# A fused transformer step on one core: where the recurrence's head norm stands beside its output gate, and how the second feed-forward's preparation is shared among the engines

## The chip, the cores and the metric

The kernel runs on one core of one Trainium2 chip. The metric is device time in microseconds (us) of one launch; lower is better. A core has a matmul engine (PE), VectorE (DVE), ScalarE (ACT), GpSimd (POOL) and SyncE (SP, which issues the DMAs here). Each works through its own instruction queue in order, and an instruction at the head of a queue that waits holds back all that stand behind it.

## The reference

One layer of a hybrid model works on 1152 tokens (128 of a context, 1024 latent) of width 1024, in float32: a half-step feed-forward, a token mixer that adds attention and a gated linear recurrence (HGRN2), and a second half-step feed-forward. The change touches the recurrence's output and the second feed-forward:

```python
f_fw = lb_h[0] + (1.0 - lb_h[0]) * jax.nn.sigmoid(heads(hf_f, HG_DK))
o_fw, s_fw = hgrn2_chunked(q_h, 1.0 - f_fw, jnp.log(f_fw), v_h, s0[:, 0])
o_bw, s_bw = hgrn2_chunked(flip(q_h), flip(1.0 - f_bw), flip(jnp.log(f_bw)), flip(v_h), s0[:, 1])
o_rec = rmsnorm(o_fw + flip(o_bw), hg_norm_g) * jax.nn.silu(heads(hgate, HG_DV))
...
merged = jax.nn.sigmoid(ga) * (o_attn @ w_up_attn) + jax.nn.sigmoid(gr) * (o_rec @ w_up_rec)
...
x = x + 0.5 * m[2] * swiglu(modulate(x, norm_g[0], m[0], m[1]), *ffn1)
x = x + m[5] * mix
x = x + 0.5 * m[8] * swiglu(modulate(x, norm_g[2], m[6], m[7]), *ffn2)
```

Here `rmsnorm` divides by the root of a mean square, and `swiglu(h, w1, w3, w2)` is `(silu(h @ w1) * (h @ w3)) @ w2`.

## The kernel before, in words

Everything lies transposed: features on the 128 partitions, tokens along the free axis, in three blocks of 384 tokens (`CW`) or, in the second feed-forward, four quarters of 288 (`QW`). A float32 product is made of three matmuls of a narrower type (L518 to L520): each operand is split into a high part, which ACT rounds off (`xh`, `wh`, `bh`, `xd`), and a low part, the subtraction `value - high` (`xl`, `wl`, `bl`), which DVE or POOL makes. `load_w` loads a weight tile into `raw` and splits it; its argument `home` says where: `"low"` makes `wh` 128x1024 on ACT and `wl` in two halves of 128x512 on DVE (L343), none makes `wl` in one piece of 128x1024 on POOL (L351).

A scheduler places the instructions: it takes the program's order and moves what has a priority ahead (`tc.high_priority`), so the order in a queue is fixed at build time and is not that of the code. A function table of ACT is loaded where the next function isn't in the one at hand (`ACT_TABLE_LOAD`); `lnexp()` (L419) asks for the table that holds both Ln and Exp.

**The recurrence** (span 800 to 1431 us). Eight heads, made as four pairs, and woven into them the projections from `h` that everything later needs: `dense_g` (24 matmuls a block, tile `mm`), closed by `sigm` (sigmoid on ACT, tile `sg`) and, for `q` (L740) and the output gate (L800), a DVE multiply of `mm` by `sg` that also frees the matmul's bank. The scan works block by block: DVE and POOL build `QP` and `KE` with decay factors `T` (at levels of 8, 16, 32 and 64 tokens), ACT copies key halves `kr`, and PE multiplies them into `lv`. Once the four half-outputs of a pair are there (`pair["no"] == 4`), `proj_gate` of that pair squares them (`osq`), and puts `norm` on the list `later`: for each of three blocks, `rec_norm` sums the squares on PE (`ops`), `rstd` takes Ln and Exp on ACT and three `scalar_tensor_tensor` on DVE (L431 to L433), and a fourth (L1108) scales the outputs `oT`. The pairs are called 0 to 3 here; the gates of the first three run beside the next pair's scan, pair 3 after the last.

**The second feed-forward** starts at 2056 us. Its first three blocks of 256 hidden features are plain (`plain_block`): units of 24 matmuls into `ps` (L518 to L520), ACT's silu `sl` (L1763) and DVE's multiply (L1774), which frees the bank. Beside the first of them runs the last quarter (`QORDER[-1]`) of the norm, `tail`: DVE `xn` (L476), ACT's modulation (L480), a store `hd`, ACT's `bh` (L487), POOL's `bl` (L488). Its tiles `xn` come from the pool that also holds `sl`. Beside the other two run `sums`: differences `hd` (L1718 to L1721, DVE) of quarters that come back by DMA (`hb`), split into `xo` (L1724 on ACT, L1728 on DVE), the operands of seven products with sums instead of eight, used from 2144 us. The down projection (2568 to 2759 us, `down_sweep`, `down_fast`) does the same in three groups of products, each in four sweeps: it accumulates in `d` (L2044), adds to `x` and `su` on DVE (L2029, L2031, L2049), and meanwhile splits the next group's `xd` (ACT L2008; L2009 on POOL and DVE) and weights `wd` (L1983).

Of the kernel before, what the change touches and what calls it, by code (L numbers as in the profile page):

```python
# [19 lines left out]
P = 128  # L20
D = 1024
KT = D // P
# [71 lines left out]
class Trunk:  # L94
# [320 lines left out]
    def alloc_h(self):  # L415
        hl = [(self.tt(F32R, f"xh{k}"), self.tt(F32R, f"xl{k}")) for k in range(KT)]
        self.xh, self.xl = zip(*hl)

    def lnexp(self):  # L419
        self.tc.keep_in_program_order(self.nc.scalar.preload_act_table_set("natural_log_exp_and_others"))  # L420

    def rstd(self, r, ps, w=CW, out=None):
# [6 lines left out]
        nc.scalar.activation(r, ps, AF.Ln, bias=self.epst)  # L429
        nc.scalar.activation(r, r, AF.Exp, scale=-0.5)  # L430
        nc.vector.scalar_tensor_tensor(t, ps, EPS, r, ALU.add, ALU.mult)  # L431
        nc.vector.scalar_tensor_tensor(t, t, -0.5, r, ALU.mult, ALU.mult)
        nc.vector.scalar_tensor_tensor(r if out is None else out, t, 1.5, r, ALU.add, ALU.mult)  # L433
# [15 lines left out]
    def norm(self, c, i):  # L449

        nc = self.nc
        lo, hi = span(c)
        cs = slice(lo, hi)
        rs = self.rs[:, cs]
        if self.mode != "mix":
            rs = self.bank("ps1", "rsp", hi - lo)
        last = self.mode == "mix"
        if last:
            with self.tc.high_priority(offset=600):
                self.stat_end(c, rs)  # L460
        else:
            self.stat_end(c, rs)
        yield
        for k in range(KT):
            t = self.fp.tile([P, hi - lo], F32, tag=self.nt[0], bufs=self.nt[1], name="xn")
# [10 lines left out]
            nc.vector.tensor_mul(t, self.x[k][:, cs], rs)  # L476
# [10 lines left out]
            nc.scalar.copy(th, t)  # L487
            nc.gpsimd.tensor_sub(tl, t, th)  # L488
            yield

    def place(self, c):
# [222 lines left out]

    def sigm(self, ps):
        s = self.fp.tile([P, CW], F32, tag="sg", bufs=3, name="sg")
        self.nc.scalar.activation(s, ps, AF.Sigmoid)
        return s

    def proj_f(self, i, h, out):  # L720
# [14 lines left out]
    def proj_q(self, i, out):  # L735
        q = out["q"] = self.tt(F32, "q")
        w = self.load_w(self.a["w_in"][i], KT, P, home="pieces" if i == 2 else "low")
        for c in ORDER:
            ps = yield from self.proj_g(w, c)
            self.nc.vector.tensor_mul(q[:, c * CW : (c + 1) * CW], ps, self.sigm(ps))  # L740
            out["nq"] = out.get("nq", 0) + 1
            yield

# [23 lines left out]
        for f in later:  # L767
            f()

    def proj_gate(self, i, p, pair):  # L770
        nc = self.nc
        oT = pair["o"]
        assert pair["no"] == 4
        w = self.load_w(self.a["w_in"][i], KT, P, home="low")
        sq = self.tt(F32, "osq")[:, :T]
        nc.scalar.activation(sq, oT[:, :T], AF.Square)
        held, normed = [], []

        def norm():
            self.lnexp()  # L780
            for b in ORDER:
                self.rec_norm(b, oT, sq)
            normed.append(1)
            for f in held:
                f()

        def put(cs, s):
            nc.gpsimd.tensor_mul(s, oT[:, cs], s)
# [7 lines left out]
        self.later.append(norm)  # L796
        for c in ORDER:
            ps = yield from self.proj_g(w, c)
            s = self.sigm(ps)
            nc.vector.tensor_mul(s, ps, s)  # L800
            f = partial(put, slice(c * CW, (c + 1) * CW), s)
            if normed:
                f()
            else:
                held.append(f)
            yield
# [8 lines left out]
    def hgrn(self):  # L815
# [10 lines left out]
        self.cnt, self.later = 0, []  # L826
# [21 lines left out]
        def work_of(h):  # L848
            p = h // 2
            work = feed(h + 1) if h + 1 < H else []  # L850
            if h and h % 2 == 0:
                work = work + [sgs.pop(), sgs.pop()] + [self.proj_gate(5 * p - 1, p - 1, pairs[p - 1])]
            while len(work) < 4 - (h == 3) + (h == H - 1):
                work.append(sgs.pop())
            return chain(*work)
# [243 lines left out]
            d["pair"]["no"] = d["pair"].get("no", 0) + 1  # L1099
            yield  # L1100

    def rec_norm(self, c, oT, sq):
# [3 lines left out]
        nc.tensor.matmul(ps, self.onesb, sq[:, cs], start=True, stop=True)  # L1106
        self.rstd(sq[:, cs], ps)
        nc.vector.scalar_tensor_tensor(oT[:, cs], oT[:, cs], self.hg, sq[:, cs], ALU.mult, ALU.mult)  # L1108

    def attn(self):  # L1110
# [4 lines left out]
        self.lnexp()  # L1115
# [949 lines left out]
    def down_fast(self, w2, X, xg, ops, made, load_x, load_h, split_h, gm, nxt):  # L2065
# [5 lines left out]
        for g, (f, n) in enumerate(GROUPS):  # L2071
            new = {} if g else X
            last = g == len(GROUPS) - 1
            for m in range(KT // 2):
# [8 lines left out]
                def after():  # L2083
                    nonlocal k
                    if xa and k in (2, 5):
                        i, t = xa.pop(0)
                        for v in range(2):
                            c = ts(v, 2 * QW)
                            self.nc.vector.tensor_add(self.x[i][:, c], t[:, c], self.x[i][:, c])
                    if m == KT // 2 - 1 and not last:  # L2090
                        for _ in range(GROUPS[g + 1][1]):
                            next(xg, None)
                    elif last:
                        for _ in range((0, 0, 1, 2, 1, 1, 1)[k]):
                            self.folds.pop(0)()
# [24 lines left out]
    def ffn_fast(self, l, gm, nxt):  # L2120
# [9 lines left out]
        sums, ops, made = iter(()), iter(()), []  # L2130
        steps = iter(()) if l else self.whole()
        for f in range(plain):
            ws = self.pre[f] if l == 0 and f < 2 else [self.load_w(self.a["w13"][l, f, j], KT, P) for j in range(2)]
            if f == 2 - l:
                for _ in steps if l == 0 else self.tail:
                    pass
# [248 lines left out]
```

## Time and profile before

| | |
|---|---|
| runs | 2859.02, 2859.55, 2859.63 us; median 2859.55 |
| profiled execution | 2853.09 us, of which the span 2851.2 us; granted clock of PE 0.995 |
| PE busy | 2767.6 us (97%) |
| DVE, ACT, POOL busy | 2034.5 (71%), 1332.4 (47%), 967.3 us (34%) |
| ACT table loads | 39, of 1283 ns each |

Times within the program are microseconds from the start of the span. Matmuls overlap in the records: one is listed as 0.34 us, and the next starts 0.17 us behind it. A row of the timeline names the start, the length, the engine, line, operation, tiles and count, and in brackets the idle time before it with the engine, tile and line that ended it. The profiled execution ran 6.46 us below the median of the runs shown.

### The profile page before, as it was taken

The numbers are of one execution on the slowest core, as the hardware profiler recorded it, in microseconds if no ns is written. First come the engines' busy times: TensorE is split into PE (matmuls) and PEld (weight loads), VectorE is DVE, ScalarE is ACT, GpSimd is POOL, SyncE is SP. The second block draws the span as 40 slices with busy tenths as digits, with TensorE's granted clock in tenths as the row PEclk, the third lists the DMA queues.
The fourth block names the chain that finished last, engine by engine and source line by source line (L and its number), as shares of the span: only waits on it lengthen the run. The fifth ranks groups of instructions, "written<-read, shape, count | busy, mean of one in ns | idle before, by whom it ended". The sixth has DMA issues, their size and how long they took to land. (4 is left out here: it accounts for less than half of the span.)

```text
span 2851.2 us, 55762 instructions
## 1 busy us (share of the span) xinstructions
PE 2767.6 (97%) x21222; PEld 2637.0 (92%) x21222; DVE 2034.5 (71%) x4430; ACT 1332.4 (47%) x2732; POOL 967.3 (34%) x1004
## 2 busy tenths in 40 slices
PE   8999999999999999999999999899999999999998
PEld 7999999999989998899998778689989999999997
DVE  7867777677678787877356777856766665568875
ACT  6523333321176677667536787731642322235332
POOL 0133232544222222222244454433443443433450
PEclk9999999999999999999999999999999999999999
DMA  6733333743112111112512001273543443347621
GB/s 258 226 129 117 131 124 121 260 171 119 60 68 68 43 62 36 65 50 74 195 61 92 18 16 36 75 246 114 174 142 116 138 159 133 112 154 212 194 100 67
DMA packets 219579, 337.65 MB, mean 118 GB/s; under 512 B 23664, under 2 KB 141360, under 8 KB 219312
## 3 DMA queue, kind: packets, MB, share of 16 engines
q1 hardware_dynamic: 219312, 334.10, 34.9%
q8 instruction: 167, 2.74, 0.4%
q14 instruction: 100, 0.82, 0.1%
HBM read 248.47 MB, written 85.54 MB: 117 GB/s over the span
## 5 line engine op out<-in xcount | busy, mean ns | idle before, releaser
L1844 PE MATMUL b<-xo,wo 128*128 128x288 f32 x3552 | 483.6, 295 | 0.8 <-DVE wo L1819 0.8
L1844 PEld LDWEIGHTS b<-xo,wo 128*128 128x128 f32 x3552 | 475.3, 188 | 1.0 <-DVE wo L1819 1.0
L1844 PE MATMUL b<-bh,wo 128*128 128x288 f32 x1776 | 366.4, 295 | 0.0
L518 PE MATMUL mm<-xh,wh 128*128 128x384 f32 x984 | 345.2, 351 | 11.9 <-DVE sg L800 6.8
L520 PE MATMUL mm<-xh,wl 128*128 128x384 f32 x984 | 334.4, 340 | 0.0
L519 PE MATMUL mm<-xl,wh 128*128 128x384 f32 x984 | 333.7, 339 | 0.0
L547 DVE SCALAR_TENSOR_TENSOR x<-dn,modt,x 128x256 f32<-128x256 f32 (+4 forms) x472 | 226.1, 499 | 89.4 <-PE dn L520 88.0
L1844 PEld LDWEIGHTS b<-bh,wo 128*128 128x128 f32 x1776 | 289.1, 188 | 0.0
L1844 PE MATMUL b<-bl,wo 128*128 128x288 f32 x888 | 262.0, 295 | 0.0
L1818 ACT CAST wo<-raw 128x512 fp32r<-128x512 f32 x185 | 114.8, 621 | 204.0 <-PE b L1844 83.0
L518 PEld LDWEIGHTS mm<-xh,wh 128*128 128x128 f32 x984 | 186.6, 190 | 20.4 <-DVE sg L800 8.2
L2044 PE MATMUL d<-xd,wd 128*128 128x288 f32 x1344 | 181.7, 297 | 9.1 <-DVE x L2031 6.4
L2044 PEld LDWEIGHTS d<-xd,wd 128*128 128x128 f32 x1344 | 180.0, 190 | 10.7 <-ACT wd L1982 3.5
L519 PEld LDWEIGHTS mm<-xl,wh 128*128 128x128 f32 x984 | 186.7, 190 | 1.1 <-issue 0.3
L520 PEld LDWEIGHTS mm<-xh,wl 128*128 128x128 f32 x984 | 186.8, 190 | 0.0
L1819 DVE TENSOR_TENSOR wo<-raw,wo 128x512 fp32r<-128x512 f32 x185 | 127.6, 691 | 71.6 <-ACT wo L1818 69.0
L1541 POOL TENSOR_TENSOR ehl<-e,ehl 128x512 fp32r<-128x512 f32 x93 | 123.9, 1337 | 153.7 <-ACT ehl L1539 85.2
L1844 PEld LDWEIGHTS b<-bl,wo 128*128 128x128 f32 x888 | 167.4, 189 | 0.0
L390 DVE SCALAR_TENSOR_TENSOR junk<-wada,cb 128x512 bf16<-128x512 f32 x224 | 162.3, 724 | 5.8 <-DMA wada<-in_w_aT 4.9
L351 POOL TENSOR_TENSOR wl<-raw,wh 128x1024 fp32r<-128x1024 f32 (+2 forms) x48 | 95.5, 1993 | 159.0 <-ACT wh L350 153.2
L1819 DVE TENSOR_TENSOR wo<-ws,wo 128x512 fp32r<-128x512 f32 x74 | 72.2, 975 | 103.1 <-ACT wo L1818 102.9
L518 PE MATMUL ps<-bh,wh 128*128 128x288 f32 (+1 forms) x448 | 136.4, 305 | 7.4 <-DVE sl L1774 4.1
(458 smaller groups left out, 7118.8 us busy)
## 6 DMA issues: line engine op xcount, KB each, us to landing
raw<-in_w SPq DMA_DIRECT2D x148, 256.0 KB, 3.3
wada<-in_w_aT SPq DMA_DIRECT2D x112, 256.0 KB, 3.0
raw<-in_w SPq DMA_DIRECT2D x42, 512.0 KB, 3.6
raw<-in_w_in SPq DMA_DIRECT2D x41, 512.0 KB, 3.3
xr<-xd SPq DMA_DIRECT2D x56, 288.0 KB, 3.8
hr<-hs SPq DMA_DIRECT2D x26, 576.0 KB, 5.6
hb<-hd SPq DMA_DIRECT2D x44, 288.0 KB, 3.4
hs<-et SPq DMA_DIRECT2D x84, 144.0 KB, 2.2
```

Of the source, the lines that this page charges most:

```text
L351: pin((eng or self.nc.gpsimd).tensor_sub(wl, raw, wh))
L390: nc.vector.scalar_tensor_tensor(junk, ws[n % 2], 1.0, cs[s], ALU.mult, ALU.mult, accum_out=o)
L518: pin(nc.tensor.matmul(ps, wh, xh, start=start and i == 0, stop=False))
L519: pin(nc.tensor.matmul(ps, wh, xl, start=False, stop=False))
L520: pin(nc.tensor.matmul(ps, wl, xh, start=False, stop=stop and i == n - 1))
L547: nc.vector.scalar_tensor_tensor(self.x[m][:, a:b], ps[:, a - lo : b - lo], self.modt[:, gm, m, s : s + 1], self.x[m][:, a:b], ALU.mult, A ...
L1541: eng.tensor_sub(el, e, eh)
L1818: nc.scalar.copy(wh, src[i])
L1819: nc.vector.tensor_sub(wl, src[i], wh)
L1844: nc.tensor.matmul(ps, w[:, k], x[:, k, :QW], start=first, stop=last, skip_group_check=home != i)
L2044: nc.tensor.matmul(ps, w[:, k], xv, start=start, stop=stop, skip_group_check=home != i)
```

## The change

Four edits, and what they do to the order.

1. **Head norm.** `norm_gate` is cut out of `proj_gate` and is called as soon as the pair's four outputs exist, beside the merge-gate projection that runs then (`beside`). `behind` adds order-only dependencies: the roots (Ln, Exp) come behind their table load, that load behind the last twelve sigmoids, and each sigmoid behind the last six roots.
2. **Gate products.** The multiplies by `sg` for `q` and for the output gate get `high_priority(offset=150)`.
3. **Start of the second feed-forward.** The tail quarter's `xn` come from the `half` tiles, its `bl` go from POOL to DVE, and the weights of plain blocks 1 and 2 are split with `home="low"`: eight halves on DVE in place of four whole ones on POOL.
4. **Down projection.** The splits of the next group's operands are asked for two per product in the last sweep of a group (before: as many as the next group has products, 3), the rest two per product in the first sweep of the next.

```diff
+    def behind(self, ins, *first):
+        for f in first:
+            self.tc.add_manual_dep(ins.ins, f.ins.name, ...)
+        return ins
...
     def sigm(self, ps):
-        self.nc.scalar.activation(s, ps, AF.Sigmoid)
+        self.sigs.append(self.behind(self.nc.scalar.activation(s, ps, AF.Sigmoid), *self.roots[-6:]))
...
     (q projection)
-            self.nc.vector.tensor_mul(q[:, c * CW : (c + 1) * CW], ps, self.sigm(ps))
+            s = self.sigm(ps)
+            with self.tc.high_priority(offset=150):
+                self.nc.vector.tensor_mul(q[:, c * CW : (c + 1) * CW], ps, s)
...
+    def norm_gate(self, pair):
+        (square, then on the list later:)
+            table = self.behind(self.lnexp(), *self.sigs[-12:])
+            for b in ORDER:
+                self.rec_norm(b, oT, sq, table)
...
+    def beside(self, work, pair):
+        for _ in work:
+            yield
+            if pair["no"] == 4 and "held" not in pair:
+                self.norm_gate(pair)
...
-                work = work + [sgs.pop(), sgs.pop()] + [self.proj_gate(5 * p - 1, p - 1, pairs[p - 1])]
+                work = work + [sgs.pop(), self.beside(sgs.pop(), pairs[p - 1])]
+                work += [self.proj_gate(5 * p - 1, p - 1, pairs[p - 1])]
...
     (norm)
+        last, tail = self.mode == "mix", i == 2 and c == QORDER[-1]
+            if tail:
+                t = self.half("xn")[:, : hi - lo]
-            nc.gpsimd.tensor_sub(tl, t, th)
+            (nc.vector if tail else nc.gpsimd).tensor_sub(tl, t, th)
...
     (plain blocks)
-            ... [self.load_w(self.a["w13"][l, f, j], KT, P) for j in range(2)]
+            ... self.load_w(self.a["w13"][l, f, j], KT, P, home="low" if l and f else None)
...
     (down_fast)
+                    if m == KT // 2 - 1 and not last or g and not m:
+                        for _ in range(2):
+                            next(xg, None)
                     if m == KT // 2 - 1 and not last:
-                        for _ in range(GROUPS[g + 1][1]):
-                            next(xg, None)
+                        pass
```

**ACT in the recurrence, gate of pair 0.** Before, the roots (`osq`) stand between sigmoids (`sg`), each with a load of its own; this stretch begins behind the copies of the key halves `kr`:

```order
L429 ACT_TABLE_LOAD
L429 ACTIVATE osq<-ops,epst 128x384 x2
L430 ACT_TABLE_LOAD
L430 ACTIVATE osq<-osq 128x384 x2
L429 ACT_TABLE_LOAD
L429 ACTIVATE osq<-ops,epst 128x384
L717 ACT_TABLE_LOAD
L717 ACTIVATE sg<-mm 128x384
L430 ACT_TABLE_LOAD
L430 ACTIVATE osq<-osq 128x384
L717 ACT_TABLE_LOAD
```

Now they stand about 14 rows earlier, right behind the transposed keys `kT`, between two loads (their lines are now L439 and L440, and the sigmoid is L730):

```order
L1094 COPY kT<-kt 128x384
L430 ACT_TABLE_LOAD
L439 ACTIVATE osq<-ops,epst 128x384 x2
L440 ACTIVATE osq<-osq 128x384 x2
L439 ACTIVATE osq<-ops,epst 128x384
L1052 COPY kr_9106<-KE 64x24x8
L440 ACTIVATE osq<-osq 128x384
L730 ACT_TABLE_LOAD
L730 ACTIVATE sg<-mm 128x384
```

Six of the eight loads around this gate go: before there is also one of L420 and one of L717 ahead of the stretch. Pairs 2 and 3 go from eight loads to two as well; pair 1 keeps its two, and its roots move ahead by the same step. In all, 39 loads become 21. On PE only the three `ops` of pairs 0 to 2 move, to right behind the transposes `kt` (in pair 1 to behind the second of three gate blocks).

**DVE at the same place.** Before, the norm's twelve `scalar_tensor_tensor` stand behind the next block's `Kb` and `Qb`, with the gate's multiply (`sg`) in their midst:

```order
L965 TENSOR_TENSOR Kb<-kk,X 64x384
L966 TENSOR_TENSOR Qb<-qx,Y 64x384
L965 TENSOR_TENSOR Kb<-kk,Y 64x384
L966 TENSOR_TENSOR Qb<-qx,X 64x384
L431 SCALAR_TENSOR_TENSOR rt<-ops,osq 128x384 x2
L432 SCALAR_TENSOR_TENSOR rt<-rt,osq 128x384 x2
L433 SCALAR_TENSOR_TENSOR osq<-rt,osq 128x384 x2
L1108 SCALAR_TENSOR_TENSOR oT<-oT,vec,osq 128x384 x2
L800 TENSOR_TENSOR sg<-mm,sg 128x384
L431 SCALAR_TENSOR_TENSOR rt<-ops,osq 128x384
```

Now they stand some twenty rows earlier, behind the factor `Gall` and ahead of `QP` at level 16, for which PE's next `lv` waits:

```order
L1078 TENSOR_TENSOR Gall<-T_12753 128x3
L441 SCALAR_TENSOR_TENSOR rt<-ops,osq 128x384 x2
L442 SCALAR_TENSOR_TENSOR rt<-rt,osq 128x384 x2
L443 SCALAR_TENSOR_TENSOR osq<-rt,osq 128x384 x2
L1138 SCALAR_TENSOR_TENSOR oT<-oT,vec,osq 128x384 x2
L441 SCALAR_TENSOR_TENSOR rt<-ops,osq 128x384
L1077 TENSOR_TENSOR QP<-QP,T_11951 64x12x16
L442 SCALAR_TENSOR_TENSOR rt<-rt,osq 128x384
L1082 COPY_PREDICATED A_0_9112<-mask,lv 128x96
L443 SCALAR_TENSOR_TENSOR osq<-rt,osq 128x384
L1085 TENSOR_TENSOR Ad<-A_0_9112,A_9114 128x96
L1138 SCALAR_TENSOR_TENSOR oT<-oT,vec,osq 128x384
```

Nine of them are ahead of `QP`, three among what follows it. The multiplies of `q` keep their places between their neighbours.

**DVE at the start of the second feed-forward**, behind the tail's `rsp`. Before, the tail's `xn` alternate with the units' multiplies `sl`, and the first `xo` follow:

```order
L476 TENSOR_TENSOR xn<-x_21843,rsp 128x288
L476 TENSOR_TENSOR xn<-x_21879,rsp 128x288
L1774 TENSOR_TENSOR sl<-ps,sl 128x288
L476 TENSOR_TENSOR xn<-x_21917,rsp 128x288
L476 TENSOR_TENSOR xn<-x_21942,rsp 128x288
L1774 TENSOR_TENSOR sl<-ps,sl 128x288
L476 TENSOR_TENSOR xn<-x_21967,rsp 128x288
L1774 TENSOR_TENSOR sl<-ps,sl 128x288
```

Now six `xn` stand ahead of the first `sl`, and from there on the low parts of the tail (L501) and of the weights (L343) stand among the multiplies:

```order
L1804 TENSOR_TENSOR sl<-ps,sl 128x288
L501 TENSOR_TENSOR bl<-xn,bh 128x288 x2
L343 TENSOR_TENSOR wl<-raw,wh 128x512
L489 TENSOR_TENSOR xn<-x_22049,rsp 128x288
L501 TENSOR_TENSOR bl<-xn,bh 128x288 x2
L489 TENSOR_TENSOR xn<-x_22074,rsp 128x288
L1804 TENSOR_TENSOR sl<-ps,sl 128x288
L501 TENSOR_TENSOR bl<-xn,bh 128x288 x2
L343 TENSOR_TENSOR wl<-raw,wh 128x512
L501 TENSOR_TENSOR bl<-xn,bh 128x288 x2
L1804 TENSOR_TENSOR sl<-ps,sl 128x288
```

On POOL eight `bl` and the four `wl` of 128x1024 are gone there, between the weight sums `wq` which stay.

In the down projection the order differs only from the first group to the second: one 128x576 `xd` fewer stands on DVE ahead of the two `x` additions (L2031 before) that end the first group's sweeps, and it follows behind them. From the second group to the third, all queues read as before.

More of the change, by code (lines that the diff above doesn't have):

```diff
@@ L428, in rstd @@
             t = self.fp.tile([P, n], F32, tag="hf", bufs=self.hfb, name="rt")[:, :w]
[L429 to L430 removed]
+        pin(nc.scalar.activation(r, ps, AF.Ln, bias=self.epst))
+        pin(nc.scalar.activation(r, r, AF.Exp, scale=-0.5))
         nc.vector.scalar_tensor_tensor(t, ps, EPS, r, ALU.add, ALU.mult)
@@ L773, in proj_gate @@
         assert pair["no"] == 4
-        w = self.load_w(self.a["w_in"][i], KT, P, home="low")
         sq = self.tt(F32, "osq")[:, :T]
         nc.scalar.activation(sq, oT[:, :T], AF.Square)
-        held, normed = [], []
+        held = pair["held"] = []
         def norm():
-            self.lnexp()
+            table = self.behind(self.lnexp(), *self.sigs[-12:])
             for b in ORDER:
-                self.rec_norm(b, oT, sq)
-            normed.append(1)
+                self.rec_norm(b, oT, sq, table)
+            pair["normed"] = 1
             for f in held:
                 f()
+        self.later.append(norm)
+    def beside(self, work, pair):
[3 more added lines that the diff above has]
+                self.norm_gate(pair)
+    def proj_gate(self, i, p, pair):
+        nc = self.nc
+        if "held" not in pair:
+            self.norm_gate(pair)
+        oT, held = pair["o"], pair["held"]
+        w = self.load_w(self.a["w_in"][i], KT, P, home="low")
         def put(cs, s):
@@ L799, in proj_gate @@
             s = self.sigm(ps)
-            nc.vector.tensor_mul(s, ps, s)
+            with self.tc.high_priority(offset=150):
+                nc.vector.tensor_mul(s, ps, s)
             f = partial(put, slice(c * CW, (c + 1) * CW), s)
-            if normed:
+            if "normed" in pair:
                 f()
@@ L825, in hgrn @@
         self.A2 = f32("A2", [P, 3, G])
-        self.cnt, self.later = 0, []
+        self.cnt, self.later, self.sigs, self.roots = 0, [], [], []
         heads = [{} for _ in range(H)]
@@ L1100, in scan_out, with rec_norm @@
             yield
-    def rec_norm(self, c, oT, sq):
+    def rec_norm(self, c, oT, sq, table):
         nc = self.nc
@@ L1106, in rec_norm @@
         nc.tensor.matmul(ps, self.onesb, sq[:, cs], start=True, stop=True)
-        self.rstd(sq[:, cs], ps)
+        self.rstd(sq[:, cs], ps, pin=lambda i: self.roots.append(self.behind(i, table)))
         nc.vector.scalar_tensor_tensor(oT[:, cs], oT[:, cs], self.hg, sq[:, cs], ALU.mult, ALU.mult)
@@ L2132, in ffn_fast @@
         for f in range(plain):
-            ws = self.pre[f] if l == 0 and f < 2 else [self.load_w(self.a["w13"][l, f, j], KT, P) for j in range(2)]
+            ws = self.pre[f] if l == 0 and f < 2 else [
+                self.load_w(self.a["w13"][l, f, j], KT, P, home="low" if l and f else None) for j in range(2)
+            ]
             if f == 2 - l:
```

18 lines of the change are left out of this document (11 added, 7 removed).

## The prediction

> **What bounds the kernel now.** I read the page first, then the chain of waits of PE in the three stretches that the change touches.
>
> ```profile
> PE 2767.6 (97%) x21222; PEld 2637.0 (92%) x21222; DVE 2034.5 (71%) x4430; ACT 1332.4 (47%) x2732; POOL 967.3 (34%) x1004
> ```
>
> PE is the bound: outside its 2767.6 us the span of 2851.2 us holds 84 us. Nothing here takes work from PE, so the change is worth only what it takes from PE's waits. They are, in the recurrence (1000 to 1431 us), at the start of the second feed-forward (2056 to 2144) and in the down sweeps (2568 to 2759), as total, times, longest:
>
> ```profile
> PE mm L518 <- DVE sg L800: 6.8, 5, 1.8
> PE mm L518 <- DVE q L740: 3.2, 2, 2.3
> PE lv L1010 <- DVE QP L1047: 2.9, 3, 1.9
> ...
> PE ps L518 <- DVE sl L1774: 4.1, 3, 2.2
> PE ps L519 <- POOL bl L488: 2.2, 4, 1.2
> PE ps L518 <- ACT bh L487: 0.4, 1, 0.4
> ...
> PE d L2044 <- DVE x L2031: 6.4, 5, 2.5
> ```
>
> That is 12.9, 6.7 and 6.4 us. A second cost hides behind the waits. In these windows the columns are length, busy time of PE, PEld, DVE, ACT and POOL, the granted clock, DMA:
>
> ```profile
> 1053.18:1056.59 3.41, 1.56 (x41) 1.21 (x41) 2.96 (x6) 3.35 (x5) 0.21 (x1) 1.00 0.02 5
> 1056.59:1060.01 3.42, 3.42 (x12) 3.42 (x12) 2.30 (x5) 3.37 (x7) 1.95 (x4) 0.50 0.00 0
> 1203.30:1207.00 3.70, 3.70 (x81) 3.57 (x77) 3.41 (x13) 3.17 (x8) 0.50 (x1) 0.54 0.02 4
> 1319.30:1322.90 3.60, 3.51 (x11) 3.51 (x12) 2.19 (x6) 3.56 (x6) 1.99 (x4) 0.53 0.00 0
> 2121.40:2125.10 3.70, 3.70 (x19) 3.70 (x18) 1.29 (x2) 1.45 (x4) 0.00 (x0) 0.54 0.13 45
> 1414.00:1420.00 6.00, 5.00 (x29) 5.01 (x30) 3.48 (x7) 4.28 (x6) 2.60 (x3) 1.00 0.10 36
> ```
>
> PE idles 1.85 us of the first window, and through the next it has half the clock: 3.42 us that do 1.7 us of work. The same happens behind the waits at 1201, 1317 and 2118 us. Behind the wait at 1413 us it does not (clock 1.00). The waits there are:
>
> ```profile
> 1056.35 0.51 PE L518 MATMUL mm<-xh,wh 128*128 128x384 f32 x1 [1.85 <-DVE sg L800]
> 1203.17 0.45 PE L1010 MATMUL lv<-QP,kr 128*32 128x32 f32 x24 [1.88 <-DVE QP L1047]
> 1319.39 0.69 PE L518 MATMUL mm<-xh,wh 128*128 128x384 f32 x1 [1.82 <-DVE sg L800]
> 1414.99 0.44 PE L518 MATMUL mm<-xh,wh 128*128 128x384 f32 x1 [1.49 <-DVE sg L800]
> 2120.22 0.40 PE L518 MATMUL ps<-bh,wh 128*128 128x288 f32 x1 [2.16 <-DVE sl L1774]
> ```
>
> So waits of 1.82 us and more cost 1.7 us on top, 1.49 us does not, and the border lies between. I count 1.7 us where a wait falls below 1.5.
>
> The Trainium skill, "TensorE: Matmul & The Clock Gate", Part 1 (The HAM clock gate), has the half clock come after an idle window of about 3.4 us. The window's length agrees with the 3.42 us above; that it has to be idle throughout does not, as PE was busy 1.56 us of it. By that rule none of my four shortened waits would bring 1.7 us, and the sum below would be 10.8 instead of 17.6.
>
> **Head norm, pairs 0 and 2.** Why `sg` is late at 1056 us, on ACT:
>
> ```profile
> 1036.09 0.48 ACT L1064 COPY kT<-kt 128x384 f32<-128x384 f32 x1
> ...
> 1047.41 1.28 ACT L429 ACT_TABLE_LOAD   x1
> 1048.70 1.06 ACT L429 ACTIVATE osq<-ops,epst 128x384 f32<-128x384 f32 x2
> 1051.07 0.94 ACT L430 ACTIVATE osq<-osq 128x384 f32<-128x384 f32 x2
> 1053.92 1.28 ACT L717 ACT_TABLE_LOAD   x1
> 1055.22 0.49 ACT L717 ACTIVATE sg<-mm 128x384 f32<-128x384 f32 x1
> ```
>
> Four loads of 1.28 us (the first and the last of them are shown) stand in front of this sigmoid with the norm's roots between them. Afterwards all of it stands between the copies of `kT` and the first sigmoid, some 10 us earlier (`kT` is copied by 1036.57): load 1.28, Ln 1.06, Exp 0.94, Ln and Exp of the third block 1.1, a copy 0.35, load 1.28 make 6.0 us in front of the first sigmoid, where two loads of 1.28 stood. From 1036.6 us that gives the sigmoid at 1042.6, done at about 1043.1; PE ends the block before `lv` at 1043.8 and needs no bank of it sooner. The sigmoid at 1055.22 is then free to run when its matmuls end.
>
> What the twelve `scalar_tensor_tensor` now delay on DVE:
>
> ```profile
> 1042.06 0.16 DVE L1048 TENSOR_TENSOR Gall<-T 128x3 f32<-128x3 f32 x1
> 1043.83 0.40 PE L1010 MATMUL lv<-QP,kr 128*32 128x32 f32 x24
> 1044.71 2.20 PE L1106 MATMUL ops<-osq,onesb 128*128 128x384 f32 x6
> 1051.63 1.02 DVE L431 SCALAR_TENSOR_TENSOR rt<-ops,osq 128x384 f32<-128x384 f32 x2 [1.10 <-ACT osq L430]
> 1054.44 1.14 DVE L1108 SCALAR_TENSOR_TENSOR oT<-oT,vec,osq 128x384 f32<-128x384 f32 x2
> 1055.74 0.56 DVE L800 TENSOR_TENSOR sg<-mm,sg 128x384 f32<-128x384 f32 x1 [0.16 <-ACT sg L717]
> ```
>
> Eight of them took 1051.63 to 1055.58, 0.49 us each. Two `KE` multiplies step back behind them, so they begin near 1041.4 instead of 1042.2; nine at 0.49 and `QP` itself put `QP` at about 1046.2. PE wants it for the next `lv`: at 1043.83, plus the `ops` that move ahead of it (1044.71 to the next matmul at 1046.46, 1.75), so 1045.5. That is a new wait of 0.8. Behind it `Ad` and its copies hold the second sigmoid (0.15), and the multiply for the third block ends with `Kb` and `Qb` in front of it (0.4). 1.85 becomes 1.35, none of them long enough for the half clock: a gain of 0.5 + 1.7 = 2.2. Bounds: a third `mm` that waits as now while the new waits are added (-1.35), and the whole 1.85 + 1.7 = 3.55. I take the worked value. `KE` and `kr`, which also step back, serve the next block's `lv`, over 10 us later. Pair 2 reads alike: 2.2.
>
> **Pair 1** had its roots together already and only moves them some 13 us earlier. The twelve no longer meet the 1.88 us wait at 1203 us, but the chain before it (reciprocals, then `QP`) stays. Bounds 0 and 1.88 + 1.7 = 3.6; I take the middle of the wait, 1.0, and with the rest below 1.5 the clock's 1.7: 2.7. **Pair 3**: its wait of 1.49 lies behind the same loads and nothing of the scan follows that could be late: 1.5 (0 to 1.5). Recurrence: 2.2 + 2.7 + 2.2 + 1.5 = **8.6**.
>
> **Gate products.** Those of `q` keep their neighbours on DVE, so the 3.2 us on L740 stay: 0. Those of the output gate are in the sum above.
>
> **Start of the second feed-forward.** POOL's whole splits are what the quarter waits behind, and DVE slows beside them:
>
> ```profile
> L351 POOL TENSOR_TENSOR wl<-raw,wh 128x1024 fp32r<-128x1024 f32 x5 | 12.9, 2581 | 15.9 <-ACT wh L350 14.2 <-issue 1.7
> L488 POOL TENSOR_TENSOR bl<-xn,bh 128x288 fp32r<-128x288 f32 x15 | 12.9, 877 | 5.7 <-ACT bh L487 5.5
> 2060.94 2.54 DVE L1721 TENSOR_TENSOR hd<-hb,hd 128x288 f32<-128x288 f32 x1
> 2060.45 0.45 DVE L1720 TENSOR_TENSOR hd<-hb,hd 128x288 f32<-128x288 f32 x1
> 2075.49 0.98 DVE L476 TENSOR_TENSOR xn<-x,rsp 128x288 f32<-128x288 f32 x2 [5.14 <-DMA hs<-sl]
> L343 DVE TENSOR_TENSOR wl<-raw,wh x74: 678/691/1403, 859.4 to 1400.1; 128x512 fp32r<-128x512 f32 x74
> ```
>
> The same subtraction of 128x288 takes 0.45 us on DVE alone and 2.54 us beside POOL's 128x1024 split. The change drops four of those (10.3 us of POOL) and adds to DVE eight halves at 0.69 (5.5 us) and eight `bl` at 0.45 (3.6 us). The quarter's `xn` wait 5.14 us for a tile that a store of `sl` frees; from the `half` tiles they need not. The 2.2 on `bl`, 0.4 on `bh`, 4.1 on `sl` and the half clock at 2121 (1.7) make 8.4. What is late next is `sl` behind `bl` and `wl` on DVE: an `sl` with two `bl` and one `wl` in front waits up to 1.6 us, and PE sees it only when its banks run out. I leave 1.0 for that: **7.4**. Bounds: 3 (the waits on `bl` and `bh` go, the others stay) and 8.4.
>
> **Down sweeps.** Only the step from the first group to the second differs:
>
> ```profile
> 2610.78 1.56 DVE L2009 TENSOR_TENSOR xd<-xr,xd 128x576 fp32r<-128x576 f32 x1
> 2613.93 0.93 DVE L2031 SCALAR_TENSOR_TENSOR x<-d,modt,x 128x288 f32<-128x288 f32 x2
> ```
>
> One such `xd` fewer stands ahead of the `x` for which PE waits: **1.6**. Bounds: 0 (the weight split beside it ends last anyway) and 3 (the next wait shortens too). From the second group to the third: 0.
>
> **Sum.** 8.6 + 7.4 + 1.6 = 17.6 us off the profiled execution's 2853.09: 2835.5. That execution lies 6.46 us below the median of the runs shown, so the forecast in the median's terms is **2842.0**.
>
> **Rivals.**
>
> (a) *DVE becomes the limit of the gates.* Beside POOL a DVE instruction stretches (2.54 for 0.45 above); then `QP` comes 2 us later than worked out, the new wait is 2.8, and it earns the half clock that it was to save. Pairs 0 and 2 then give nothing, pair 1 about 1: the recurrence 2.5, the sum 11.5, time 2848.1. For it: nine instructions ahead of `QP` where PE has 3 us of room. Against it: POOL is nearly idle in the window at 1053 (0.21 us).
>
> (b) *The half clock stays.* It depends on where waits fall in windows of 3.41 us; if the four that I count off reappear elsewhere, 6.8 us go: 10.8 left, time 2848.8. For it: another wait of 2.3 (`q`) is still there, and shifted work meets other windows.
>
> (c) *A switch of tables costs more than its load.* If each load were followed by a pause as long again (1.28), the first sigmoid of pairs 0 and 2 would come 2.6 us later than worked out, and PE would wait about 2.2 for it; pairs 0 and 2 would give nothing, the recurrence 4.2, the sum 13.2, time 2846.4. Against it: the load at 1047.41 ends at 1048.69 and the next instruction starts at 1048.70. The Trainium skill, "ScalarE: Activation LUTs", What ACT_TABLE_LOAD costs, gives about 1283 ns for the load and 1380 ns of drain with each switch; the load agrees with the 1.28 here, and no row here shows the drain.
>
> (d) *Slower: DVE stands at the head of its queue for `wh`.* POOL waited 14.2 us on ACT's `wh` in front of its splits, where nobody stood behind. On DVE the `sl` of the units, `hd` and `xo` stand behind it. If DVE inherits the whole 14.2 and its own 5.5 and PE feels all of it, that edit costs 19.7 and the total is -19.7 + 8.6 + 1.6 = 9.5 slower: 2869. It decides from a loss of 16 us there (10.2 + 5.7). Against it: the halves stand behind instructions that themselves wait for the same units, so `wh` is mostly done.
>
> (e) *Little is changed*: table loads and splits come off engines that were idle anyhow, and PE's waits move to the next instruction. Every wait above then keeps 80% of its length: gain 3.5, time 2856.
>
> **How the numbers follow.** The forecast 0.62 (its own range 2837 to 2847), (a) 0.12, (b) 0.11, (c) 0.03, (e) 0.08, (d) 0.04. The range reaches from the sum of the upper bounds (3.55 + 3.6 + 3.55 + 1.5 + 8.4 + 3 = 23.6, or 2836) to 2853, over (a) to (c) with four microseconds of their own; it leaves out (d), (e) and the tails. A measurement of this kernel can tell about 0.2%, 5.7 us, from no change. Faster by more: the forecast and (a) to (c), 0.88; within: (e), 0.08; slower: (d), 0.04.
>
> **What would show it.** Right: 21 table loads; no half clock near 1057, 1203 and 1319; the five waits on `sg` (6.8) down to under 3; POOL without 128x1024 splits between 2065 and 2110 and no `hd` or `xo` of over 1 us there; the wait on `bl` gone. Wrong: `lv` waiting for `QP` over 1.5 us in pairs 0 and 2 (a); half clocks at new places (b); an ACT pause behind loads (c); `ps` waiting for `sl` over 5 us in all (d).

## The result, and the profile after

The changed kernel ran 2838.51 us in the median (2835.16 to 2842.20, 4 runs) against 2859.38 (2859.02 to 2859.63) of the kernel before on that chip: a ratio of 0.9928, 95% interval 0.9913 to 0.9944. On a second chip it ran 2838.02 against 2854.09: 0.9942 (0.9930 to 0.9954). The forecast was 2842.0, range 2836 to 2853. Its profiled execution took 2837.95 us, the span 2836.2, 15.0 less than before.

The page of the changed kernel, and what PE waited for in the recurrence (1000 to 1431 us), at the start of the second feed-forward (2050 to 2143) and in the down sweeps (2560 to 2755), as total, times, longest:

```profile
PE 2760.5 (97%) x21222; PEld 2630.5 (93%) x21222; DVE 2034.8 (72%) x4446; ACT 1309.2 (46%) x2714; POOL 950.3 (34%) x992
...
PE mm L531 <- DVE q L755: 4.3, 3, 2.3
PE lv L1040 <- DVE QP L1077: 3.1, 4, 1.4
PE ops L1136 <- ACT kT L1094: 1.8, 2, 0.9
PE mm L531 <- DVE sg L829: 1.4, 3, 0.8
PE dS L1102 <- ACT kT L1094: 1.1, 1, 1.1
PE vt L773 <- ACT t L766: 0.7, 1, 0.7
PE ops L1136 <- ACT osq L790: 0.5, 1, 0.5
...
PE ps L531 <- ACT sl L1793: 1.0, 1, 1.0
PE nps L515 <- DVE rs L457: 0.9, 1, 0.9
PE ps L531 <- DVE sl L1804: 0.7, 1, 0.7
...
PE d L2074 <- DVE x L2061: 4.2, 4, 2.5
PE d L2074 <- DVE su L2079: 2.0, 1, 2.0
```

The waits on `sg` fell from 6.8 to 1.4 us; those on `q` rose from 3.2 to 4.3, and 2.3 us of waits at `ops` are new. With the small rows counted too, all waits of the recurrence fell only from 14.6 to 12.9 us. At the start of the feed-forward 6.7 us became 2.6, and no `bl` is among them. PE's busy time fell by 7.1 us at the same 21222 matmuls: that is mostly half clock, which the records count as busy. Before the last matmuls there were seven windows of 3.41 us at half clock, and there are four now: two near 820 us (one before), and those near 1100 us and in the down sweeps that both kernels have. Of the four places at half clock that the prediction counted, none is left; three of them, with length, the five engines' busy times, the granted clock, DMA share and GB/s:

```profile
1053.00:1060.00 7.00, 7.00 (x74) 6.65 (x73) 6.71 (x12) 3.20 (x9) 3.81 (x5) 1.00 0.32 105
1200.00:1207.00 7.00, 5.56 (x99) 5.19 (x98) 6.60 (x18) 5.52 (x13) 1.50 (x4) 1.00 0.01 2
1316.00:1323.00 7.00, 7.00 (x73) 6.65 (x72) 6.74 (x10) 2.89 (x9) 5.24 (x6) 1.00 0.41 131
```

To see where the 15 us went, the start of the same matmul is compared in both traces (after minus before, `ops` and `kt` left out of the count):

| stretch (us of before) | at its start | at its end | gained | forecast |
|---|---|---|---|---|
| up to the recurrence, 0 to 1030 | 0 | +1.2 | -1.2 | 0 |
| pair 0, 1030 to 1110 | +1.2 | -0.5 | 1.7 | 2.2 |
| pair 1, 1150 to 1225 | -0.5 | -0.3 | -0.2 | 2.7 |
| pair 2, 1295 to 1350 | -0.3 | -2.8 | 2.5 | 2.2 |
| pair 3, 1412 to 1460 | -2.8 | -5.05 | 2.2 | 1.5 |
| second feed-forward's start, 2056 to 2143 | -5.0 | -12.2 | 7.2 | 7.4 |
| its seven-product blocks, 2143 to 2560 | -12.2 | -12.75 | 0.6 | 0 |
| down sweeps, 2560 to 2716 | -12.75 | -14.85 | 2.1 | 1.6 |

One trace stands behind each row, and two traces of one kernel differ. In `all`, the changed kernel once more (below), the first row is a gain of 1.7 instead of a loss of 1.2, pairs 0 to 3 give 1.6, -1.0, 2.5 and 2.0, and the start of the feed-forward gives 8.3.

Pair 0 in the changed kernel, on ACT, then DVE, then PE:

```profile
1037.20 0.48 ACT L1094 COPY kT<-kt 128x384 f32<-128x384 f32 x1
1037.70 1.28 ACT L430 ACT_TABLE_LOAD   x1
...
1042.02 1.28 ACT L730 ACT_TABLE_LOAD   x1
1043.31 0.49 ACT L730 ACTIVATE sg<-mm 128x384 f32<-128x384 f32 x1
...
1052.91 0.49 ACT L730 ACTIVATE sg<-mm 128x384 f32<-128x384 f32 x1
...
1042.21 1.02 DVE L441 SCALAR_TENSOR_TENSOR rt<-ops,osq 128x384 f32<-128x384 f32 x2
...
1046.98 0.36 DVE L1077 TENSOR_TENSOR QP<-QP,T 64x192 f32<-64x192 f32 x1
...
1037.73 0.91 PE L1136 MATMUL ops<-osq,onesb 128*128 128x384 f32 x2 [0.90 <-ACT kT L1094]
1048.03 0.40 PE L1040 MATMUL lv<-QP,kr 128*32 128x32 f32 x24
```

The roots stand between two loads. The sigmoid that ran at 1055.22 before runs at 1052.91, with its table long loaded. This trace runs 1.2 us behind that of before here (first row of the table), so `QP`, which ended at 1047.3, came when the prediction had it (1046.2 in the time of before). Yet `lv` does not wait: PE itself came to it only at 1048.03, some 1.3 us later than the prediction had. Of these, 0.90 is a new wait, since the third `ops` needs a bank that ACT's copy of `kT` frees. Rival (a)'s long wait of `lv` is not there (0.6 us at most in pairs 0 and 2), nor is rival (c)'s pause: the load at 1037.70 ends at 1038.98, and the next instruction starts at 1038.99.

At the start of the feed-forward POOL has one 128x1024 split left (block 0's), and DVE's subtractions there shrank. POOL's row and DVE's `xo` after, then DVE's `xo` before:

```profile
L351 POOL TENSOR_TENSOR wl<-raw,wh 128x1024 fp32r<-128x1024 f32 x1 | 2.4, 2397 | 0.3 <-POOL bl L501 0.3
...
L1758 DVE TENSOR_TENSOR xo<-hd,xo 128x288 fp32r<-128x288 f32 x32 | 15.6, 527 | 0.0
```

```profile
L1728 DVE TENSOR_TENSOR xo<-hd,xo 128x288 fp32r<-128x288 f32 x32 | 21.1, 706 | 0.0
```

The same 32 subtractions of `xo` took 21.1 us before and 15.6 after, and the difference pays for the 5.4 us of weight halves that DVE took over. Their means, 706 and 527 ns, mix. Before, 18 of the 32 met nothing on POOL and took 0.45 us each; two beside its 128x1024 splits took 2.09 and 2.62, three beside its `bl` 1.05, the others beside its smaller work 0.44 to 0.99. After, none meets a big split or a `bl`, and the longest takes 0.99.

### The profile page after: what moved, and what is told of

It reads as the page before. It is cut to its first block, busy times and chain, and to the rows that moved or that the text cites. A ratio compares the mean times of both kernels' runs of the same rounds, so it can differ in the third digit from the quotient of the medians.

```text
span 2836.2 us, 55733 instructions
## 1 busy us (share of the span) xinstructions
PE 2760.5 (97%) x21222; PEld 2630.5 (93%) x21222; DVE 2034.8 (72%) x4446; ACT 1309.2 (46%) x2714; POOL 950.3 (34%) x992
## 5 line engine op out<-in xcount | busy, mean ns | idle before, releaser
L1848 ACT CAST wo<-ws 128x512 fp32r<-128x512 f32 x74 | 45.6, 618 | 214.6 <-POOL ws L1844 214.5
```

Of the source, the lines that this page charges most:

```text
L1848: nc.scalar.copy(wh, src[i])
```

## The experiments

All are timed against the kernel before on their chip; the third column is the ratio's distance from 1 times that median.

| kernel | ratio (95%) | us against before | profiled execution |
|---|---|---|---|
| norm: edits 1 and 2 | 0.9969 (0.9958 to 0.9980) | -8.9 (-12.0 to -5.7) | 2849.37 |
| tables: norm at its old place | 0.9978 (0.9969 to 0.9987) | -6.3 (-8.9 to -3.7) | 2848.41 |
| early: place without batching | 0.9991 (0.9983 to 1.0000) | -2.6 (-4.9 to 0.0) | 2852.09 |
| ffn: edit 3 | 0.9970 (0.9958 to 0.9982) | -8.6 (-12.0 to -5.1) | 2844.57 |
| wl: weights' half of edit 3 | 0.9971 (0.9961 to 0.9981) | -8.3 (-11.1 to -5.4) | 2850.09 |
| tail: quarter's half of edit 3 | 0.9983 (0.9975 to 0.9992) | -4.9 (-7.1 to -2.3) | 2847.64 |
| down: edit 4 | 0.9996 (0.9987 to 1.0004) | -1.1 (-3.7 to +1.1) | 2854.05 |
| all: the changed kernel | 0.9942 (0.9930 to 0.9954) | -16.6 (-20.0 to -13.1) | 2838.02 |
| nop1: all, pair 1 at its old place | 0.9944 (0.9932 to 0.9957) | -16.0 (-19.4 to -12.3) | 2839.39 |
| qrec: all, reciprocals behind `q` | 0.9952 (0.9939 to 0.9965) | -13.7 (-17.4 to -10.0) | 2838.50 |
| fill: before, 9 transposes at four places | 1.0000 (0.9992 to 1.0009) | 0.0 (-2.3 to +2.6) | 2854.01 |
| fill2: the same at two places | 0.9991 (0.9982 to 1.0000) | -2.6 (-5.1 to 0.0) | 2853.44 |

The kernel before ran 2850.5 to 2860.9 us over the 70 runs beside these. The interval of one part is so wide that stretches of the traces, not totals, tell the parts apart.

**norm.** The second feed-forward and the down sweeps are put back:

```diff
-        last, tail = self.mode == "mix", i == 2 and c == QORDER[-1]
+        last, tail = self.mode == "mix", False
-                ... home="low" if l and f else None
+                ... home=None
```

> Edits 1 and 2 alone (head norm and gate products; second feed-forward as before). Theory: the recurrence keeps what the changed kernel shows there, PE 6.2 us earlier at 1460 us, of which 5.1 are three half-clock stretches that go; nothing after it differs, so the profiled execution gains about 6 to 7 us and the median as much. Rival (the parts need each other): under 3 us alone. Rival (the 6 us by which the median of before lies above its profiled execution come from the same waits): the median gains 10 us or more, the profile 6.

From 1030 to 1460 us PE gains 6.3 in its trace (from -0.25 to -6.54), as the changed kernel does (6.2). The median's gain of 8.9 (5.7 to 12.0) allows the theory and not the first rival; it does not exclude the second at its lower end.

**tables and early** take edit 1 apart.

```diff
(tables)
-                work = work + [sgs.pop(), self.beside(sgs.pop(), pairs[p - 1])]
+                work = work + [sgs.pop(), sgs.pop()]
(early, in behind)
-        for f in first:
+        for f in ():
```

> As norm, but the norm is asked for where it was before, so the three ops stand at their old places; only the roots' batching (21 loads in place of 39) is left. Theory: loads are the cause of the late gate sigmoids in pairs 0, 2 and 3, so this alone gives the 1.5 of pair 3 and half or more of pairs 0 and 2, 3 to 6 us. Rival: the batch itself (three roots before any sigmoid) holds the third block's sigmoid as long as before, and the earlier place is what counts: pairs 0 and 2 give 0, the gain is 1.5 to 2 us.

> Edits 1 and 2 without the order-only dependencies: the norm stands where the changed kernel has it, but the table is loaded as the scheduler happens to mix roots and sigmoids (37 loads in place of 21). Theory: loads are what the gain hangs on in pair 3, the earlier place in pairs 0 and 2; pair 3 gives 0, pairs 0 and 2 some 1 us each: 1 to 4 us better than before, 3 to 6 worse than with the dependencies (7.4). Rival: the place alone carries it, 6 us or more better than before.

Batching alone gains 4.1 of the 6.3 us between 1030 and 1460 in its trace (-0.92 to -4.99): 2.5 in pair 3, 1.3 in pair 2, 0.6 in pair 0, and -0.4 in pair 1. The place alone gains 0.6 (+0.50 to -0.10): 1.8 in pair 0 and 2.4 in pair 2, as much as both together give there, but -2.9 in pair 1 and -0.7 in pair 3. In pair 1 eight table loads now stand between 1148 and 1171 us where before had two, ACT's `ohi` waits for POOL's product ahead of the copies that PE needs, and a half clock follows near 1195 us; which of these costs how much is not shown. The waits of `early` on DVE's gate products, and its ACT at pair 1:

```profile
PE mm L531 <- DVE sg L829: 5.3, 3, 1.9
...
1194.78 0.51 ACT L819 CAST ohi<-sg 128x384 fp32r<-128x384 f32 x1 [5.85 <-POOL sg L817]
```

So pairs 0 and 2 owe more to the place than I had expected, pair 3 owes all to the batching, and without the binding pair 1 takes most of it back: 5.3 us of waits on `sg` where `norm` has 1.4.

**ffn, wl, tail** take edit 3 alone and apart.

```diff
(wl)
+                self.load_w(..., home="low" if l and f else None)
(tail)
+                t = self.half("xn")[:, : hi - lo]
+            (nc.vector if tail else nc.gpsimd).tensor_sub(tl, t, th)
```

> Edit 3 alone (tail quarter in its own tiles with its low parts on DVE, weights of plain blocks 1 and 2 split on DVE). Theory: the stretch from 2056 to 2143 us gives the 7.2 us it gives in the changed kernel, and the recurrence is as before: 7 us. Rival: the gain there depends on the earlier shift against the clock's windows, and the half clock near 2121 stays: 5.5 us.

> Before with one half of edit 3: the weights of plain blocks 1 and 2 split on DVE in halves; the tail quarter as before. Theory: this half takes POOL's 128x1024 splits away from beside DVE and brings the waits on sl (3.4 us at 2110 and 2118) and the half clock there, 3 to 5 of the 7 us. Rival: the tail's own tiles bring it all, this half 0 to 1.

> Before with the other half of edit 3: the tail quarter's xn in the half tiles and its low parts on DVE, weights as before. Theory: the stretch from 2068 to 2090 us gives its 5 us (waits on bl, bh and sl there), the waits at 2110 and 2118 stay, 2.5 to 4 us in all. Rival: with POOL's 128x1024 splits still beside it DVE is slow with bl too, 0 to 1.

From 2056 to 2143 us `ffn` gains 5.3 in its trace (+0.55 to -4.75) and keeps the half clock behind a wait of 2.4 us on `sl`, as its rival said; in the changed kernel that wait is under 1. What shortens it there is not shown. `wl` gains 6.0, nearly all at 2110 and 2118; `tail` gains 5.3 between 2068 and 2090 and gives 1.1 back behind. Their waits in that stretch, `wl` first, then `tail`:

```profile
PE ps L519 <- POOL bl L488: 1.8, 1, 1.8
PE ps L518 <- DVE sl L1774: 0.5, 1, 0.5
```

```profile
PE ps L521 <- DVE sl L1777: 5.7, 2, 3.0
```

Each half removes the waits that it was expected to remove (the split on DVE those on `sl`, the tail's tiles those on `bl`). For `wl` the median gained more than expected (5.4 to 11.1, expected 3 to 5). Together they bring less than 6.0 + 4.2: with the tail alone, the waits on `sl` grow from 4.1 to 5.7. I take the reason to be that PE comes sooner to units whose multiplies are still late; no run tests it. Differences of 1 or 2 us between these gains mean little: the six kernels that leave this stretch alone (`norm`, `tables`, `early`, `down`, `fill`, `fill2`) move by -2.1 to +1.6 in it. All gains here are well above that.

**down.**

```diff
-                    if m == KT // 2 - 1 and not last:
-                        for _ in range(GROUPS[g + 1][1]):
-                            next(xg, None)
+                    if m == KT // 2 - 1 and not last or g and not m:
+                        for _ in range(2):
+                            next(xg, None)
```

> Edit 4 alone. Theory: only the step from the first group to the second changes, 1.6 to 2.1 us. Rival: the weight split beside the removed operand split ends last anyway, 0. Rival: the later splits come too late for the second group, slower by 1 to 2 us.

From 2560 to 2660 us its trace gains 2.3 (+4.68 to +2.40), but this sum can't be put down to the edit: `ffn`, whose down projection is that of before, gains 2.3 there too, and the seven others without edit 4 between -1.5 and +1.6. What the edit does is seen at the `d` that waits for the `x` additions at the end of the first group, before and then in `down`:

```profile
2614.59 0.64 PE L2044 MATMUL d<-xd,wd 128*128 128x288 f32 x3 [2.05 <-DVE x L2031]
```

```profile
2617.54 0.64 PE L2044 MATMUL d<-xd,wd 128*128 128x288 f32 x3 [0.90 <-DVE x L2031]
```

In the nine traces without the edit this wait lasts 2.02 to 2.07 us, in the five with it 0.82 to 0.90. So 1.2 us are the edit's, near the theory's lower end. The median's -1.1 (-3.7 to +1.1) cannot tell that from 0, and no loss as the second rival feared is in the trace.

**all and nop1.** The changed kernel again, and with pair 1 left where it was:

```diff
-                ... self.beside(sgs.pop(), pairs[p - 1])]
+                ... self.beside(sgs.pop(), pairs[p - 1]) if p != 2 else sgs.pop()]
```

> The changed kernel again, on the chip of the next three. The profiles so far show half-clock stretches at places that differ from run to run, each behind a window of 3.41 us in which PE idled about 1.6 us or more. Theory: the parts add up, 7.4 + 7.1 + 0.4 = 14.9 us below before, with runs that spread by some 6 us. Rival: they help each other, 18 us or more.

> The changed kernel with pair 1 asked for at its old place (its three ops stand where they stood before). Theory: what pair 1 gains at 1201 us is paid at the roots' new place (1.4 us) and by the next wait on q at 1221 us, so leaving it costs nothing: within 1 us of the changed kernel (2838.0). Rival: its wait of 1.9 us and its half clock count, 2 to 3 us slower than the changed kernel.

The parts' medians add to 18.6 (8.9 + 8.6 + 1.1), `all` gives 16.6: within the intervals they add up, and neither the theory's 14.9 nor 18 is excluded. `nop1` is 0.6 us from `all`: pair 1's early place is worth nothing that can be seen, with intervals of some 3.5 us either way. In the traces pair 1 gives -0.3 in `nop1`, against -0.2 and -1.0 with the early place.

**qrec** puts the scan's reciprocals behind the products for `q`:

```diff
-        nc.vector.reciprocal(X[:, :, 4:8], Y[:, :, 4:8])
+        self.behind(nc.vector.reciprocal(X[:, :, 4:8], Y[:, :, 4:8]), *self.qs[-1:])
```

and the same for the other reciprocal; `self.qs` collects the products.

> The changed kernel, and both reciprocals of the scan's preparation are put behind the last q product asked for, so that the three q products per head pair stand ahead of them on DVE. Theory: PE's waits on q (4.3 us in the changed kernel, 2.3 the longest, with a half clock behind it) go, 3 to 6 us better than the changed kernel. Rival: DVE is the limit there, the reciprocals then come late for QP and lv waits instead: 0 to 1 us.

The waits on `q` are gone, and in the same scan (1000 to 1431 us) PE waits for ACT and others instead:

```profile
PE ops L1136 <- ACT kT L1094: 4.5, 2, 2.5
PE vt L773 <- ACT t L766: 3.9, 3, 2.4
PE ops L1136 <- ACT osq L790: 2.5, 1, 2.5
PE lv L1040 <- DVE QP L1077: 1.5, 2, 1.1
```

12.4 us of waits here against 12.9 in the changed kernel. Ahead of this window, from 895 to 985 us, the trace of `qrec` loses another 6.0 us: `lv` waits 2.8 for `QP` between 850 and 1000 (0.5 in the changed kernel), 2.5 the longest, with two windows at half clock behind it. It wins most of that back where the waits on `q` stood. The rival was right, in the total and in where the wait would go: no gain. No version tried is better than the changed kernel.

**fill and fill2** add work to PE and take no wait away: the three transposes `kt` in front of the 1.85 and 1.82 us waits are made four times into the same tile.

```diff
-        for j in range(3):
-            nc.tensor.transpose(pt[:, j], KE[:, ts(j, P)], self.ident)
+        for _ in range(4 if nth in (8, 20) else 1):
+            for j in range(3):
+                nc.tensor.transpose(pt[:, j], KE[:, ts(j, P)], self.ident)
```

In `fill` the number `nth` was kept per head rather than per block, so the extra transposes also stood one block earlier.

> Before, with nine more transposes of 128x128 (each of the three made four times into the same tile) in front of the two waits of 1.85 and 1.82 us in pairs 0 and 2; no wait is removed. Theory (half clock follows a window half idle): PE idles about 0.6 there instead of 1.8, both half-clock stretches go whatever the windows' phase, the waits end when they ended; the profile gains up to 3.4 us at these places, the median 1.7 to 3.4, although PE does more. Rival (a whole idle window is needed, the slow stretches have another cause): the stretches stay, no gain, or a loss of up to 2 us.

> As fill, but the extra transposes stand only at the two places in front of the waits of 1.85 and 1.82 us (in fill they also stood one block earlier, where PE does not wait). Theory: no half clock near 1057 and 1319, the two waits end when they ended; the profile gains up to 3.4 us there and the median about half of that (1.7), since only some phases of the windows hold the whole wait. Rival: 0, or a loss of what the extra work adds (up to 2.5 us).

In `fill2` the window before the place is busy 2.58 us where it was 1.56, and the clock stays whole behind it:

```profile
1053.18:1056.59 3.41, 2.58 (x46) 2.25 (x41) 2.52 (x5) 3.35 (x5) 0.64 (x1) 1.00 0.02 5
1056.60:1060.00 3.40, 3.40 (x21) 3.40 (x20) 2.69 (x6) 3.33 (x7) 1.93 (x4) 1.00 0.00 0
```

Laid out from the half clocks of `fill2` itself, its window is 1053.64 to 1057.05, busy 2.58 us too, and without the transposes the whole wait would lie in it. Nor is there half clock near 1319 in either kernel. PE gains 1.6 us against before from 1053 to 1062, and gives 1.4 back by 1070: it waits 1.14 us for the next gate product at 1061.52. The transposes are not the reason. `wl`, whose recurrence is that of before, has no half clock at 1057 in its execution either; it gains the same 1.6 us and loses it at the same matmul:

```profile
1062.31 0.45 PE L518 MATMUL mm<-xh,wh 128*128 128x384 f32 x1 [1.12 <-DVE sg L800]
```

In before the half clock fills this wait, so taking it away alone is worth next to nothing here, and the medians are flat or nearly so (0.0, and -2.6 with an interval that ends at 0). That less idle time of PE keeps the clock whole is shown at these two places; that it gains time is not.

## Why the prediction was right, and where it was not

**The head norm** was forecast at 8.6 and gave 6.2 in the trace (5.0 in that of `all`). The reason held: loads stood in front of the gates' sigmoids. `tables` (21 loads, old place) shows it, and pair 3, where nothing else changed, gained even the 0.5 us wait behind it that I had not counted. On DVE `QP` came when I had worked it out, but the new wait of pairs 0 and 2 is at `ops` (0.9 us, a bank freed by `kT`), not at `lv` behind `QP`.

**Pairs 0 and 2** came out near their 2.2 (1.7 and 2.5), and that is partly luck. Of each 2.2 the sum took 1.7 for the half clock, as a cost by itself. `wl` and `tail` leave the recurrence alone; from 1030 to 1460 us `wl` has no half clock at 1057, 1203 or 1319, `tail` none at the last two, and they gain nothing (-0.15 and -0.1): without the half clock PE only comes sooner to a gate product that is late as well (the wait of 1.12 us above). The changed kernel keeps the gain because that product comes sooner too: it ran at 1061.35 before and at 1059.65 now, 2.9 us sooner once the 1.2 between the traces is taken off. The sum had no such term; behind the first product it counted only new waits (0.15 and 0.4).

**Pair 1 is the term that failed**: 2.7 forecast, -0.2 measured. The step was the same, to count a wait and its half clock as gone without asking what stands behind. The half clock went, and the wait at 1201 us shrank from 1.88 to 1.44. But the new place cost 1.5 us of waits at 1158 to 1180 (on `osq` and `QP`), and the next wait swallowed the rest. DVE there, before and then after:

```profile
1218.93 1.35 DVE L960 RECIPROCAL X<-Y 128x192 f32<-128x192 f32 x1
1221.03 1.05 DVE L958 RECIPROCAL Y<-X 128x144 f32<-128x144 f32 x1
1222.00 0.49 DVE L740 TENSOR_TENSOR q<-mm,sg 128x384 f32<-128x384 f32 x1
```

```profile
1218.66 1.35 DVE L990 RECIPROCAL X<-Y 128x192 f32<-128x192 f32 x1
1220.78 1.05 DVE L988 RECIPROCAL Y<-X 128x144 f32<-128x144 f32 x1
1221.75 0.49 DVE L755 TENSOR_TENSOR q<-mm,sg 128x384 f32<-128x384 f32 x1
```

PE arrived 1.9 us earlier, the product of `q` only 0.25: DVE's chain sets the time here, so PE waited 1.1 us where it had not before, and 1.6 of the 1.9 were lost. `tables`, `tail` and `wl` show the same step: they are 1.3 us sooner at 1210 and lose 1.6 by 1225. `tail` and `wl` change nothing there; in their executions the half clock at 1203 was missing, so even that was worth nothing by 1225.

**The gate products** of `q` stay where they were: 0, as forecast from the order.

**The start of the feed-forward** was forecast at 7.4 and gave 7.2, for the reasons given: waits on `bl` and `bh` gone, those on `sl` from 4.1 to 0.7 us, the half clock at 2121 gone. DVE waited 1.2 us on `wh` in all (rival d feared 14.2). **The down sweeps** were forecast at 1.6 and gave 2.1 in the table, of which 1.2 is shown to be the edit's.

**The half clock** was forecast at 1.7 us for each of four waits, with a border between 1.49 and 1.82 us of wait. The four half clocks are gone, but that the length of a wait decides was wrong: in the trace of before itself, waits of 2.05 us at 2614 and 2.03 at 2697 have whole clock behind them. Here rival (b) had a point: what counts is PE's idle time within a window of 3.41 us, and the windows' phase differs from execution to execution. Nor is the price always 1.7: it was next to nothing in the recurrence, as above. At 2121 it was real: `fill2`, whose feed-forward is that of before, has the same wait of 2.16 us and no half clock, and gains 1.5 us there. In `down`, which does not touch the recurrence, the wait of pair 3 lasted 1.84 us instead of 1.49 and half clock followed, so neither is a property of the place:

```profile
1412.84:1416.26 3.42, 1.58 (x9) 1.25 (x8) 2.21 (x5) 3.38 (x4) 0.92 (x1) 1.00 0.20 80
1416.26:1419.67 3.41, 3.41 (x13) 3.41 (x12) 2.76 (x5) 2.37 (x4) 1.04 (x2) 0.50 0.04 16
```

In each trace all half clocks start a whole number of windows of 3.413 us apart, so every trace's windows can be laid out from its own half clocks. Over the fourteen traces, from the first clock record (19 us) to the last matmuls, 80 windows at whole clock were followed by one at half clock. In 76 of them PE idled 1.57 us or more, in four 1.13 to 1.44. Every window with more than 1.87 us idle was followed by half clock; with 1.57 to 1.87, 26 were not. So the border lies near half the window, and these records do not place it closer. The Trainium skill, "TensorE: Matmul & The Clock Gate", Part 1 (The HAM clock gate), calls the window free-running, which these phases agree with, and has the half clock come after an idle window of about 3.4 us, which here only some of those near 820 us and at the program's end had in front.

**The 6.46 us** between the profiled execution and the median of the runs shown I carried over as an offset. It is not one: 70 later runs of the kernel before spread over 10 us, with medians of 2854 to 2855 on three chips, and the changed kernel's profiled execution (2837.95) lies 0.6 us below its median. The forecast came 3.5 us above the result because the trace-based sum (2835.5) erred by -2.5, mostly pair 1 and the first row of the table, and this offset by 5.9 the other way. That the two errors partly cancel is luck. I take the moving windows as the cause of the spread; executions without a profile do not show their clock, so that stays argued.

## What to carry to other kernels

Where one engine alternates between functions of two tables, bind the order so that one batch stands between two loads: here the bound batch at its old place gave 4.1 us of 6.3, and the moved roots without the binding 0.6. Before counting a wait as gained, find the next place where the bounding engine meets a chain that is not its own; a microsecond won ahead of such a place is lost there, be it a wait or a stretch of half clock that goes. A subtraction that goes from one engine to another also changes the speed of what runs beside it, so price both.

## What the runs showed of the hardware that was not expected

PE's half clock followed when about half of a 3.41 us window was idle (1.57 us or more in 76 of 80 cases), with a phase that differs between executions, so the same wait brings 3.41 us of half clock in one run and none in another; `fill2` removed it by adding work. What it costs depends on what waits behind it: 1.5 us at 2121, nothing to 0.2 in the recurrence. The 128x288 subtractions `xo` took 0.45 us each on DVE beside no work of POOL, 1.05 beside its 128x288 `bl`, and 2.09 and 2.62 beside its 128x1024 splits.
